# Decoder trunk with dilated attention: K and Q of a head in one transfer each, V's raw tiles ahead of them, and another order of a head's loads

## The chip, the cores and the metric

The kernel runs on one core of a Trainium2 chip. The metric is the device time of one execution in microseconds (us), lower is better. Times before are the median of three runs.

## The reference

A decoder trunk of two layers on one sequence of 1024 positions and 1024 features, in float32. Layer 0 mixes with a short gated convolution, layer 1 with dilated attention; a SwiGLU block (2816 wide) follows each, and a final RMSNorm ends it. The change lies in the attention.

```python
BRANCHES = ((128, 1), (512, 4), (2048, 16))      # window, dilation
...
def dilated_attention_mixer(h, w_qkv, w_out, rel_bias):
    qkv = (h @ w_qkv).reshape(bsz, seq, 3, N_HEADS, HEAD_DIM)   # 16 heads of 64
    q, k, v = qkv[:, :, 0], qkv[:, :, 1], qkv[:, :, 2]
    outs, lses = [], []
    for window, dilation in BRANCHES:
        o, l = dilated_branch(q, k, v, rel_bias, window, dilation)
        outs.append(o)
        lses.append(l)
    alpha = jax.nn.softmax(jnp.stack(lses, axis=0), axis=0)
    o = jnp.sum(alpha[..., None] * jnp.stack(outs, axis=0), axis=0)
    return o.reshape(bsz, seq, D_MODEL).astype(h.dtype) @ w_out
...
def dilated_branch(...):      # banded causal attention over each strided subsequence
    s = einsum(qb, kk) * (HEAD_DIM ** -0.5)
    s = where(mask, s + bias, NEG_INF)
    lse = logsumexp(s, axis=-1)
    o = einsum(exp(s - lse[..., None]), vv)
```

Query t sees the keys t - j x dilation for j = 0 to window/dilation, with a learned bias by distance and head.

## The kernel before, in words

**Numbers.** Each float32 operand of a matmul is split in two parts, hi (a copy on ScalarE, L169 for weights) and lo (a subtraction on VectorE, L170), and a product is three matmuls: hi by hi, hi by lo, lo by hi. Where the keys and queries meet, K's page holds both parts of a head (64 partitions each), so that one matmul with Q's hi part twice (L1789) and one with Q's lo part beside zeros (L1790) do it.

**Memory.** SBUF is a ring of 41 pages of 128 x 1024 float32, with half pages beside them. A tile that needs a page waits until the old holder's last reader is done. Scratch in DRAM carries the projections on: `kq[p, part]`, one tensor of 256 x 1024 for each pair of heads p and part (0 is Q, 1 is K), with the hi rows of both heads in 0 to 127 and the lo rows in 128 to 255; `vdram`, the values.

**Queues.** The order of all work is written by hand, and each engine runs its own instructions in program order. Loads are issued on SyncE (SP), in program order: a load that waits for a page holds up those behind it. Scratch stores are issued on GpSimd (POOL). Weights come as raw tiles (`load_raw`, L201 and L204), are split when `ensure` reaches them and handed out by `take`.

**Q and K.** `QueryKey` computes the projections with a seven-product scheme; `emit` writes each half page of the result as hi (L1288) and lo (L1291) to `kq`, 32 stores of each kind, between about 985 and 1105 us.

**V.** `mix` goes on with V. Its first ten heads come by seven products as well (`value_products` in the order 1, 5, 6, 7, 4, 3, 2, five of them in `mix`); the rest, the plain part of V, by eight `value_tiles` of plain matmuls, from four raw tiles of 128 x 768 numbers that come in eight transfers. Those raw tiles (index `raw_v` on) are loaded during product 3, or on demand. The loads of K and Q of head 0 (`self.first = load_rows(self, 0)`) are issued after product 4.

**Attention.** A loop over 16 heads runs `slot(n)`. Slot n issues the loads for head n + 1 (`load_kq`: K's page `ka` in two loads of 64 rows, L1240 and L1241; Q's page `qa` in two loads of the same 64 rows, one for each half of the partitions, L1243; Q's lo part `ql`, L1767; then the bias table in two loads, L1704 and L1705), computes the scores of head n (L1789, L1790, bias added on VectorE from L1800 on), starts its softmax, and multiplies the probabilities of head n - 1 with V (L1865), whose four tiles for a pair of heads (`class0`, `class1`, `keys0`, `keys1`, one buffer each) are loaded by `load_values` (L1758). ScalarE makes a regrouped copy `kca` of K (`classes`, L1773). For n below EVEN = 11 a slot is cut in eight even steps i; the value products of head n - 1 start in step 4 of slot n and end in steps 0 to 3 of slot n + 1; the V tiles of pair p are loaded in steps 0 to 3 of slot 2p + 1, in the order of VBLOCKS. From slot 11 on another order applies. Between these, `dense` work fills TensorE: the two late products of V and the value tiles, later the output projection (`out_product`), in units handed out by `other(k)`; DENSE says how many a slot gets.

The source of L1704, the bias table's first part, is a pattern `[[1, 8], [A1, 16], [1, L1]]`, that of L1705 `[[1, 32], [A2, 4], [1, L2]]`.

Of the kernel before, what the change touches and what calls it, by code (L numbers as in the profile page):

```python
# [10 lines left out]
F32 = mybir.dt.float32  # L11
# [6 lines left out]
S = 1024  # L18
D = 1024
DF = 2816  # L20
H = 16
KT = D // 128
# [50 lines left out]
EVEN, VALUES_BEFORE = 11, 17  # L73
EVEN_SOFT = (2, 1, 1, 1, 1, 1, 0, 0)
EVEN_PV = (3, 2, 2, 2, 2, 2, 2, 1)
VBLOCKS = ("class0", "class1", "keys0", "keys1")
OIN = LAG - 3
DENSE = (19, 12) + (7,) * 8 + (6, 10, 10, 12, 10, 9, 8)
DEEP_ORDER = (1, 2, 5, 6, 7, 3, 4)
# [46 lines left out]
def trunk(ctx: ExitStack, tc: tile.TileContext, x, gains_in, cwi, ck, cwo, wqkv, wo, relb,  # L126
# [19 lines left out]
    def half(h):  # L146
        return slice(h * HALF, (h + 1) * HALF)
# [44 lines left out]
    def load_raw(upto):  # L192
        while raw_state[0] < min(upto + 1, len(raw_src)):
            i, at = raw_state[0], 0
            raw_tile[i] = page("raw")
            src = raw_src[i]
            if isinstance(src, list):
                row = width(src) // 2
                for s in src:
                    n = s.shape[2]  # L200
                    nc.sync.dma_start(view(raw_tile[i], at, [[row, 2], [1, n]]), s)  # L201
                    at += n
            else:
                nc.sync.dma_start(raw_tile[i][:, :width([src])], src)  # L204
            raw_state[0] += 1
# [1022 lines left out]
    by_time = lambda t: view(t, 0, [[1, 16], [16, 32]])  # L1228
    by_residue = lambda t: view(t, 0, [[32, 16], [1, 32]])

    def rows(t, r):
        return bass.AP(t.tensor, t.offset + r * S, [[S, 64], [1, S]])

    def load_rows(qk, n):

        p, a = divmod(n, 2)
        k, q = qk.kq[p, 1], qk.kq[p, 0]
        n0, n1 = (slice(64 * i, 64 * i + 64) for i in (a, 1 - a))
        ks, qs = page("ka", F32R), page("qa", F32R)
        nc.sync.dma_start(ks[n0].bitcast(F32), rows(k, 64 * a))  # L1240
        nc.sync.dma_start(ks[n1].bitcast(F32), rows(k, 128 + 64 * a))  # L1241
        for m in (n0, n1):
            nc.sync.dma_start(qs[m].bitcast(F32), rows(q, 64 * a))  # L1243
        return ks, qs

    vdram = [dram.tile([S, w], F32, name=f"vdram{g}") for g, w in enumerate((2 * VW, VREST))]
# [1 line left out]
    class QueryKey(Conv):  # L1248
# [28 lines left out]
        def emit(self, p, part, h, v):  # L1277

            t, rstd = half_page("kq"), self.norm.rstd[:, half(h)]
            if part == 1:  # L1280
                nc.vector.tensor_tensor(out=by_time(t), in0=by_residue(v), in1=by_residue(rstd), op=ALU.mult)
            else:
                nc.vector.scalar_tensor_tensor(t, v, 0.125, rstd, op0=ALU.mult, op1=ALU.mult)
            yield
            to = self.kq[p, part]
            hi, lo = half_page("kq_hi", F32R), half_page("kq_lo", F32R)
            nc.scalar.activation(hi, t, AF.Copy)
            nc.gpsimd.dma_start(to[:128, half(h)], hi.bitcast(F32))  # L1288
            yield
            nc.vector.tensor_tensor(out=lo, in0=t, in1=hi, op=ALU.subtract)  # L1290
            nc.gpsimd.dma_start(to[128:, half(h)], lo.bitcast(F32))  # L1291

        def out(self, u, c, v):
            self.waiting.append(self.emit(u, 1 - c[0], c[1], v))
# [85 lines left out]
        def value_product(self, m, banks, ahead=0, ws=None):  # L1380

            for j in range(4):
                whi, wlo = ws[j] if ws else take(("m", ("V", j), m), ahead)
                bhi, blo = self.b[m][j]
                for t in range(4):
                    b, s, new = banks[t][:, :VW], slice(t * 128, t * 128 + 128), j == 0 and m not in (6, 7, 4)
                    nc.tensor.matmul(b, bhi[:, s], whi, start=new, stop=False, skip_group_check=True)
                    nc.tensor.matmul(b, bhi[:, s], wlo, start=False, stop=False, skip_group_check=True)
                    nc.tensor.matmul(b, blo[:, s], whi, start=False, stop=j == 3, skip_group_check=True)
                    yield  # L1390
                if m == 2 and j == 1:
                    self.stores.pop()()
                if m == 3 and j:
                    ensure(op_state[1] + j - 1)
                    load_raw(raw_v + j)
                if m == 1 or m in VALUES[:5] and j % 2:
                    self.step(1)
                if m == 6:
                    self.x12.append(half_page("x12"))
                    nc.sync.dma_start(self.x12[j], spill[j][:, half(1)])  # L1400
                elif m == 4:
                    self.operand(8, j, j, self.x12[j])
            v, c = self.v, {1: (1, 0), 5: 5, 6: (1, 1), 7: (0, 1), 4: (0, 0), 3: (1, 1), 2: (1, 0)}[m]
            if c not in v:
                v[c] = [page("v") for i in range(2)]
            part = lambda c, t: v[c][t // 2][:, half(t % 2)][:, :VW]
            for t in range(4):
                n = t + 4 * (c == 5 or c[1])
                o, scale = part(c, t), self.norm.r[:, n:n + 1]
                if m in (1, 5, 4):  # L1410
                    nc.scalar.activation(o, banks[t][:, :VW], AF.Identity, scale=scale)
                else:
                    old = part(5, t) if m in (6, 7) else o
                    nc.vector.scalar_tensor_tensor(o, banks[t][:, :VW], scale, old, op0=ALU.mult, op1=ALU.add)
            def store():
                for i in range(2):
                    self.store_values(0, v[c][i], c[1], 2 * i, c[0] * VW, VW)
                del v[c]

            if m in (3, 2):  # L1420
                self.stores.append(store)
            elif m in (7, 4):
                store()
            if m == 7:
                del v[5]
            yield
# [287 lines left out]
    def attention(norm, qk):  # L1714
# [10 lines left out]
        def value_tiles():  # L1725

            for t in range(KT):
# [15 lines left out]
                nc.scalar.activation(v[:, half(t % 2)][:, :VREST], b, AF.Identity, scale=norm.r[:, t:t + 1])  # L1743
                if t % 2:
                    qk.store_values(1, v, j, b4 - 1, 0, VREST)
                if t > KT - 3:
                    ensure(op_state[1] + t - KT + 2)
                yield
# [10 lines left out]

        def load_kq(n):  # L1760

            p, a = divmod(n, 2)
            n0 = slice(64 * a, 64 * a + 64)
            KS[n], QS[n] = load_rows(qk, n) if n else qk.first
            if EVEN + 1 < n <= LAG + 1 and n % 2 == 0:
                load_values(p - 1)
            nc.sync.dma_start(qlo[a][n0].bitcast(F32), rows(qk.kq[p, 0], 128 + 64 * a))  # L1767

        def classes(n):

# [171 lines left out]
        def slot(n, dense, ndense, late=0):  # L1942
# [10 lines left out]
            else:  # L1953
                sc = iter(())
            if n + 1 < H:
                load_kq(n + 1)
                bias[n + 1] = load_bias(n + 1)
            if n == OIN:
                for k in range(2):
                    load_x(k)  # L1960
# [19 lines left out]
            if n < EVEN:  # L1980
                for i in range(8):
# [6 lines left out]
                    other(ndense * (i + 1) // 8 - ndense * i // 8)  # L1988
                    if i == 3:
                        run(begun)  # L1990
                    if a and p and i < 4:
                        load_values(p, VBLOCKS[i:i + 1])
                    if ending and i == 4:
                        run(ending.pop())
                    if n == 0 and i == 2:
# [26 lines left out]
                        run(ending.pop())  # L2022
                run(sc)
            else:
                if a == 0 and not late:
                    other(1)
                    used += 1
                for i in range(8):
                    next(sc, None)
                    next(pv, None)  # L2030
# [53 lines left out]
                    add_to_x(n, {c: b})  # L2084

        X[:] = [None] * KT
        bias = {0: load_bias(0)}
        load_kq(0)
        late = chain(qk.late_products(), value_tiles())
        early = classes(0)  # L2090
        for i in range(VALUES_BEFORE):
# [232 lines left out]
```

## Time and profile before

| | |
|---|---|
| runs | 2072.16, 2073.15, 2073.94 us; median 2073.15 |
| profiled execution | 2074.61 us, its span 2072.8 us |
| TensorE (PE) busy | 2050.5 us (99% of the span) |
| VectorE (DVE) busy | 1806.3 us (87%) |
| ScalarE (ACT) busy | 1062.8 us (51%) |
| GpSimd (POOL) busy | 295.8 us (14%) |
| SP's hardware queue q1 | 201.15 MB, 31.9% of 16 engines' span |
| GpSimd's software queue q0 | 90.50 MB, 15.1% |

The span is that of the instructions of one profiled execution. TensorE is busy for almost all of it, so a wait elsewhere counts only where TensorE waits as well. The page names groups by line, engine, operation and tiles (`ql<-kq` is a load from `kq` into `ql`). A releaser in a row of waits is the event that came last by the profile; where several conditions share a semaphore, another may have been meant.

### The profile page before, as it was taken

The page shows a single profiled execution, that of the slowest core. Times are in us where ns is not written, and L with a number is a line of the kernel's source. Part 1 is how long each engine was busy: PE and PEld are TensorE (multiplying, and loading weights), DVE is VectorE, ACT ScalarE, POOL GpSimd, SP SyncE. Part 2 cuts the span into 40 slices and gives each one's busy share as a digit, 9 for nine tenths or more (in the row PEclk, how much of TensorE's full clock was granted, in tenths as well). Part 3 has the DMA queues.
Part 4 walks back from the last instruction along what each step waited for, and adds up shares of the span by engine and source line. Part 5 has one row for each costly group of instructions (what it writes and reads, how often), then busy time and mean ns, then how long its engine had stood idle before and what let it go on. Part 6 is the DMA issues. An engine that isn't in the chain of part 4 may idle for free.

```text
span 2072.8 us, 30544 instructions
## 1 busy us (share of the span) xinstructions
PE 2050.5 (99%) x10642; PEld 1766.4 (85%) x10642; DVE 1806.3 (87%) x3369; ACT 1062.8 (51%) x1993; POOL 295.8 (14%) x418
## 2 busy tenths in 40 slices
PE   9999999999999999999999999999999999999998
PEld 7888888888888888888889999988888888888887
DVE  8899899988888888799976999988998888897897
ACT  7433477443444555356544577665544434355444
POOL 1011011100101021020322433211011001012000
PEclk9999999999999999999999999999999999999999
DMA  7333583233333577453745978855223323378533
GB/s 223 92 111 123 158 223 72 102 112 99 115 104 105 176 237 207 157 134 111 249 163 148 236 173 212 220 173 148 71 96 104 107 97 117 102 269 225 180 98 97
DMA packets 137033, 308.30 MB, mean 149 GB/s; under 512 B 17596, under 2 KB 45582, under 8 KB 136880
## 3 DMA queue, kind: packets, MB, share of 16 engines
q1 hardware_dynamic: 96368, 201.15, 31.9%
q0 software_dynamic: 32880, 90.50, 15.1%
q10 hardware_dynamic: 7632, 14.70, 1.9%
q8 instruction: 84, 1.38, 0.3%
q14 instruction: 69, 0.57, 0.1%
HBM read 210.78 MB, written 85.29 MB: 143 GB/s over the span
## 4 chain that ended last, share of the span: by engine, by line
PE 92%; DVE 3%; DMA 3%; ACT 1%; issue 1%; SPq 0%; DVEq 0%; ACTq 0%
PE bank L652 24%; PE bank L650 24%; PE bank L651 24%; PE bank L1865 4%; PE bank L746 3%; PE bank L749 3%; PE bank L748 3%; PE bank L451 1%; PE bank L453 1%; PE bank L452 1%; PE bank L1790 1%; PE bank L1789 1%; DMA ql<-kq 1%; DMA raw<-in_conv_w_in 1%; DMA x<-in_x 0%
## 5 line engine op out<-in xcount | busy, mean ns | idle before, releaser
L650 PE MATMUL bank<-b,w 128*128 128x512 f32 (+1 forms) x2264 | 875.8, 387 | 4.0 <-ACT w L169 2.0
L652 PE MATMUL bank<-b,w 128*128 128x512 f32 (+1 forms) x2264 | 875.2, 387 | 2.1 <-DVE w L170 1.9
L651 PE MATMUL bank<-b,w 128*128 128x512 f32 (+1 forms) x2264 | 875.3, 387 | 0.3 <-DVE b L1018 0.3
L650 PEld LDWEIGHTS bank<-b,w 128*128 128x128 f32 x2264 | 425.8, 188 | 90.5 <-ACT w L169 2.4
L652 PEld LDWEIGHTS bank<-b,w 128*128 128x128 f32 x2264 | 425.7, 188 | 90.1 <-DVE w L170 4.2
L651 PEld LDWEIGHTS bank<-b,w 128*128 128x128 f32 x2264 | 425.8, 188 | 84.7 <-DVE b L1018 0.8
L169 ACT ACTIVATE w<-combo 128x512 fp32r<-128x512 f32 (+3 forms) x528 | 279.6, 555 | 293.4 <-DVE combo L242 248.5
L170 DVE TENSOR_TENSOR w<-combo,w 128x512 fp32r<-128x512 f32 (+3 forms) x528 | 309.2, 598 | 36.5 <-ACT w L169 36.1
L656 ACT ACTIVATE part<-bank 128x512 f32<-128x512 f32 x193 | 115.1, 597 | 394.1 <-PE bank L652 386.6
L170 DVE TENSOR_TENSOR w<-raw,w 128x512 fp32r<-128x512 f32 (+3 forms) x340 | 191.1, 583 | 39.6 <-ACT w L169 39.3
L660 DVE TENSOR_TENSOR part<-part,bank 128x256 f32<-128x256 f32 (+1 forms) x371 | 174.0, 498 | 31.6 <-PE bank L652 20.8
L169 ACT ACTIVATE w<-raw 128x512 fp32r<-128x512 f32 (+3 forms) x340 | 172.5, 539 | 22.3 <-PE bank L749 10.5
L642 DVE TENSOR_TENSOR b<-hin,b 128x512 fp32r<-128x512 f32 x175 | 118.7, 685 | 16.3 <-ACT b L641 14.7
L912 DVE TENSOR_TENSOR x<-x,bank 128x512 f32<-128x512 f32 x144 | 98.4, 683 | 33.5 <-PE bank L652 31.5
L242 DVE TENSOR_TENSOR combo<-raw 128x512 f32<-128x512 f32 (+2 forms) x192 | 127.4, 664 | 0.0
L641 ACT ACTIVATE b<-hin 128x512 fp32r<-128x512 f32 x175 | 107.1, 619 | 16.0 <-DMA hin<-part 11.7
L749 PE MATMUL bank<-b,w 128*128 128x256 f32 x288 | 81.5, 283 | 0.0
L748 PE MATMUL bank<-b,w 128*128 128x256 f32 x288 | 81.5, 283 | 0.0
L746 PE MATMUL bank<-b,w 128*128 128x256 f32 x288 | 81.3, 282 | 0.0
L861 POOL DMA_DIRECT2D part<-sum x88 | 47.7, 542 | 190.5 <-DVE sum L825 115.7
L1542 DVE TENSOR_TENSOR part<-part 128x512 f32<-128x512 f32 x66 | 43.5, 686 | 28.8 <-ACT part L1527 28.8
L242 DVE TENSOR_TENSOR combo<-combo,raw 128x512 f32<-128x512 f32 (+2 forms) x96 | 64.5, 672 | 3.8 <-DMA raw<-in_conv_w_in 1.0
(252 smaller groups left out, 3075.4 us busy)
## 6 DMA issues: line engine op xcount, KB each, us to landing
hin<-part SPq DMA_DIRECT2D x154, 256.0 KB
raw<-in_ffn_w_gate SPq DMA_DIRECT2D x44, 512.0 KB
raw<-in_ffn_w_up SPq DMA_DIRECT2D x44, 512.0 KB
part<-sum POOLq DMA_DIRECT2D x88, 256.0 KB, 2.3
raw<-in_ffn_w_down SPq DMA_DIRECT2D x32, 512.0 KB
raw<-in_conv_w_in SPq DMA_DIRECT2D x24, 512.0 KB
part<-part POOLq DMA_DIRECT2D x44, 256.0 KB, 2.5
raw<-in_attn_w_qkv SPq DMA_DIRECT2D x19, 512.0 KB
```

The source lines that it names most:

```text
L169: nc.scalar.activation(hi, src, AF.Copy)
L170: low = lambda: eng.tensor_tensor(out=lo, in0=src, in1=hi, op=ALU.subtract)
L242: eng.tensor_tensor(out=c, in0=a, in1=b, op=op)
L642: return lambda: eng.tensor_tensor(out=lo, in0=t, in1=hi, op=ALU.subtract)
L650: nc.tensor.matmul(b, hi[:, a], bhi, start=start and k == 0, stop=False, skip_group_check=True)
L651: nc.tensor.matmul(b, hi[:, a], blo, start=False, stop=False, skip_group_check=True)
L652: nc.tensor.matmul(b, lo[:, a], bhi, start=False, stop=k == n - 1, skip_group_check=True)
L656: nc.scalar.activation(t, b, AF.Copy)
L660: nc.vector.tensor_tensor(out=t, in0=t, in1=b, op=ALU.add)
L746: nc.tensor.matmul(b, hi[:, a], bhi, start=i in (1, 2, 5) and k == 0, stop=False, skip_group_check=True)
L748: nc.tensor.matmul(b, hi[:, a], blo, start=False, stop=False, skip_group_check=True)
L749: nc.tensor.matmul(b, lo[:, a], bhi, start=False, stop=k == n - 1, skip_group_check=True)
```

## The change

1. **Layout of `kq`.** In each 256-row tensor the rows of the first head of a pair are now hi 0 to 63, lo 64 to 127; those of the second head lo 128 to 191, hi 192 to 255. The hi store of a half page writes two blocks of 64 rows 192 rows apart, the lo store two adjoining blocks.
2. **K and Q.** A head's K page is one load of 128 adjoining rows. Its Q page is one load from a pattern that reads the same 64 rows twice, by a leading dimension of 2 with step 0.
3. **Raw tiles of V's plain part.** The four are loaded in product 4, one after each of its operand steps, and so ahead of K and Q of head 0 on SP; before, they were asked for in product 3. The raw tile after them (the first of the output projection) is asked for after the sixth value tile.
4. **V's tiles** of a pair are loaded in the order class0, keys0, class1, keys1, at steps 0, 2, 3 and 4.
5. **`ql` and the bias** get a function of their own, `load_low`. In slots 1 to 10 it is called at step 3, in later slots at the start as before; K and Q of the next head are still issued at the slot's start. All loads for heads 0 and 1 are issued before slot 0.
6. **Dense fill.** After LAG, slot 15 gets two units of `dense` work ahead of its scores and slot 16 one; before, slot 16 alone got one.

```diff
-VBLOCKS = ("class0", "class1", "keys0", "keys1")
+VBLOCKS = ("class0", "keys0", "class1", "keys1")
+VSTEP = dict(class0=0, keys0=2, class1=3, keys1=4)
...
     def load_rows(qk, n):
 
         p, a = divmod(n, 2)
         k, q = qk.kq[p, 1], qk.kq[p, 0]
-        n0, n1 = (slice(64 * i, 64 * i + 64) for i in (a, 1 - a))
         ks, qs = page("ka", F32R), page("qa", F32R)
-        nc.sync.dma_start(ks[n0].bitcast(F32), rows(k, 64 * a))
-        nc.sync.dma_start(ks[n1].bitcast(F32), rows(k, 128 + 64 * a))
-        for m in (n0, n1):
-            nc.sync.dma_start(qs[m].bitcast(F32), rows(q, 64 * a))
+        nc.sync.dma_start(ks.bitcast(F32), k[128 * a:128 * a + 128])
+        nc.sync.dma_start(qs.bitcast(F32), bass.AP(q.tensor, q.offset + 192 * a * S, [[0, 2], [S, 64], [1, S]]))
         return ks, qs
...
             nc.scalar.activation(hi, t, AF.Copy)
-            nc.gpsimd.dma_start(to[:128, half(h)], hi.bitcast(F32))
+            place = lambda r, step: bass.AP(to.tensor, to.offset + r * S + h * HALF, [[step * S, 2], [S, 64], [1, HALF]])
+            nc.gpsimd.dma_start(place(0, 192), hi.bitcast(F32))
             yield
             nc.vector.tensor_tensor(out=lo, in0=t, in1=hi, op=ALU.subtract)
-            nc.gpsimd.dma_start(to[128:, half(h)], lo.bitcast(F32))
+            nc.gpsimd.dma_start(place(64, 64), lo.bitcast(F32))
...
                 if m == 3 and j:
                     ensure(op_state[1] + j - 1)
-                    load_raw(raw_v + j)
...
                 elif m == 4:
                     self.operand(8, j, j, self.x12[j])
+                    load_raw(raw_v + j)
...
+                if t == KT - 3:
+                    load_raw(raw_v + 4)
                 if t > KT - 3:
                     ensure(op_state[1] + t - KT + 2)
...
         def load_kq(n):
 
-            p, a = divmod(n, 2)
-            n0 = slice(64 * a, 64 * a + 64)
             KS[n], QS[n] = load_rows(qk, n) if n else qk.first
             if EVEN + 1 < n <= LAG + 1 and n % 2 == 0:
-                load_values(p - 1)
-            nc.sync.dma_start(qlo[a][n0].bitcast(F32), rows(qk.kq[p, 0], 128 + 64 * a))
+                load_values(n // 2 - 1)
+
+        def load_low(n):
+
+            p, a = divmod(n, 2)
+            nc.sync.dma_start(qlo[a][64 * a:64 * a + 64].bitcast(F32), qk.kq[p, 0][64 + 64 * a:128 + 64 * a])
+            bias[n] = load_bias(n)
...
             if n + 1 < H:
-                load_kq(n + 1)
-                bias[n + 1] = load_bias(n + 1)
+                if n:
+                    load_kq(n + 1)
+                if n >= EVEN:
+                    load_low(n + 1)
...
-                    if a and p and i < 4:
-                        load_values(p, VBLOCKS[i:i + 1])
+                    if n and i == 3:
+                        load_low(n + 1)
+                    if a and p:
+                        load_values(p, [v for v in VBLOCKS if VSTEP[v] == i])
...
-                if a == 0 and not late:
-                    other(1)
-                    used += 1
+                if n >= H - 1:
+                    other(2 if n < H else 1)
+                    used += 2 if n < H else 1
...
-        bias = {0: load_bias(0)}
+        bias = {}
         load_kq(0)
+        load_low(0)
+        load_kq(1)
+        load_low(1)
```

More of the change, by code (lines that the diff above doesn't have):

```diff
@@ L1229, in trunk @@
     by_residue = lambda t: view(t, 0, [[32, 16], [1, 32]])
-    def rows(t, r):
-        return bass.AP(t.tensor, t.offset + r * S, [[S, 64], [1, S]])
     def load_rows(qk, n):
```

## The prediction

> **What bounds the kernel now.** First the page: the busy line and the chain that ended last.
>
> ```profile
> span 2072.8 us, 30544 instructions
> PE 2050.5 (99%) x10642; PEld 1766.4 (85%) x10642; DVE 1806.3 (87%) x3369; ACT 1062.8 (51%) x1993; POOL 295.8 (14%) x418
> PE 92%; DVE 3%; DMA 3%; ACT 1%; issue 1%; SPq 0%; DVEq 0%; ACTq 0%
> ```
>
> TensorE is busy for 99% of the span, so a change of loads can win only idle time of TensorE or time at a lower clock. All that the change touches lies between 985 and 1392 us, so I next asked for windows there. Their columns are start:end, length, busy time of each engine, granted clock, busy share of the 16 DMA engines, and GB/s.
>
> ```profile
> core 0: us, PE busy (x) PEld busy (x) DVE busy (x) ACT busy (x) POOL busy (x), PEclk, DMA share, GB/s
> 18.00:22.00 4.00, 4.00 (x20) 3.30 (x19) 2.70 (x5) 2.03 (x4) 0.00 (x0) 1.00 1.04 410
> 985.00:1105.00 120.00, 119.47 (x539) 98.96 (x539) 104.90 (x166) 55.47 (x98) 34.56 (x64) 1.00 0.63 212
> 1141.16:1153.51 12.35, 12.06 (x88) 11.85 (x87) 9.12 (x19) 4.50 (x5) 6.05 (x9) 1.00 1.07 308
> 1153.51:1292.89 139.38, 133.29 (x1028) 130.97 (x1027) 137.78 (x266) 95.70 (x145) 51.70 (x43) 0.99 0.80 195
> 1292.89:1364.75 71.86, 71.86 (x504) 66.39 (x502) 62.14 (x124) 43.22 (x66) 20.30 (x12) 1.00 0.74 207
> ```
>
> A head's slot begins with its first product of K and Q (L1789). The second window is the store stage of K and Q, the third is slot 0, the fourth slots 1 to 10, the fifth slots 11 to 14:
>
> ```profile
> 1141.16 0.28 PE L1789 MATMUL bank<-qa,kca 128*128 128x256 f32 x1
> 1153.51 0.28 PE L1789 MATMUL bank<-qa,kca 128*128 128x256 f32 x1
> 1292.89 0.28 PE L1789 MATMUL bank<-qa,kca 128*128 128x256 f32 x1
> 1364.75 0.28 PE L1789 MATMUL bank<-qa,kca 128*128 128x256 f32 x1
> ```
>
> Slots 1 to 10 take 139.38/10 = 13.94 us each. In them VectorE is busy for 137.78 us of 139.38, and the DMA engines for 0.80 of the time on average. Three resources are close to full, and TensorE's waits are small. The waits of TensorE from 1100 to 1400 us, and VectorE's longest from 1140 to 1320 us (total, times, longest):
>
> ```profile
> PE bank L1865 <- DMA v_class<-vdram: 2.4, 3, 1.6
> PE bank L1790 <- DMA ql<-kq: 1.7, 2, 1.2
> PE bank L1865 <- ACT o L1888: 1.4, 1, 1.4
> PE bank L1865 <- ACT lf L1854: 0.9, 1, 0.9
> PE bank L1789 <- DMA qa<-kq: 0.4, 1, 0.4
> PE bank L1790 <- DMA raw<-in_attn_w_qkv: 0.3, 1, 0.3
> ...
> DVE w_lo L170 <- DMA ql<-kq: 1.7, 1, 1.7
> ```
>
> That is 7.1 us in all. The third is a wait for `v_keys` as well: in the program the instruction needs that load and a tile of exponentials, and ACT's `o` only shares its semaphore. Slots 1 to 10 also lose to the clock, after the longest wait for `ql`:
>
> ```profile
> 1168.59 0.39 PE L1790 MATMUL bank<-ql,kca 128*128 128x256 f32 x1 [1.19 <-DMA ql<-kq]
> 1168.00:1170.00 2.00, 1.41 (x9) 1.41 (x10) 2.00 (x6) 1.98 (x5) 1.92 (x1) 0.83 1.04 228
> 1170.00:1172.00 2.00, 2.00 (x11) 2.00 (x11) 1.97 (x4) 0.89 (x2) 1.11 (x1) 0.50 0.79 184
> 1172.00:1174.00 2.00, 2.00 (x16) 2.00 (x15) 2.00 (x5) 0.69 (x2) 1.04 (x1) 0.82 0.85 158
> ```
>
> Three windows of 2 us at 0.83, 0.50 and 0.82 lose (0.17 + 0.50 + 0.18) x 2 = 1.7 us. So everything that better loads could give is 7.1 + 1.7 = 8.8 us, less what VectorE takes in their place.
>
> **Merged K and Q (the part that decides).** SP's issues for head 0, with start and duration, and the page's sizes:
>
> ```profile
> 1128.72 0.54 SPq L1240 DMA_DIRECT2D ka<-kq  x1
> 1129.94 1.24 SPq L1243 DMA_DIRECT2D qa<-kq  x2
> 1136.35 5.76 SPq L201 DMA_DIRECT2D raw<-in_attn_w_qkv  x8
> ...
> ka<-kq SPq DMA_DIRECT2D x32, 256.0 KB
> qa<-kq SPq DMA_DIRECT2D x32, 256.0 KB
> ```
>
> Four issues become two, which saves 0.54 + 0.62 = 1.2 us of SP per head. I cost it at nothing: SP is not what TensorE waits for, and the bytes are the same. K is then one load whose source leads with 128 rows. Q is different. It must land twice, once for each half of the partitions, and the new source says so with a leading dimension of 2 (step zero), ahead of 64 rows. What does a short leading dimension cost? One load of the kernel has one: L1704, the first part of the bias table, leads with 8; the second part, L1705, leads with 32. The last pair of them stands alone on SP's queue for over 11 us:
>
> ```profile
> 1342.37 0.62 SPq L1704 DMA_DIRECT2D bias<-tables  x1
> 1343.04 0.55 SPq L1705 DMA_DIRECT2D bias<-tables  x1
> 1354.43 0.55 SPq L1758 DMA_DIRECT2D v_class<-vdram  x1
> ...
> 1344.00:1346.40 2.40, 2.40 (x21) 2.27 (x20) 2.40 (x5) 1.02 (x2) 1.54 (x1) 1.00 1.03 230
> 1346.50:1347.50 1.00, 1.00 (x11) 1.00 (x10) 1.00 (x2) 0.97 (x3) 0.00 (x0) 1.00 0.55 96
> 1347.50:1348.50 1.00, 1.00 (x8) 0.87 (x7) 1.00 (x3) 1.00 (x3) 0.00 (x0) 1.00 0.50 164
> ```
>
> While the older loads drain, all engines are busy (1.03). Then the share falls to 0.55 and 0.50 and stays there: half of the engines go on, the others have nothing left. I read this as L1704 handed out by its leading dimension, 8 pieces to 8 of 16 engines. By the same reading Q's load goes to 2 engines. The bounds are 16 engines (like the 64-row loads) and 2; the nearest row is L1704's, so I take 2.
>
> The Trainium skill, "DMA: Bandwidth & Descriptors", section "Rules for kernel authors", states this outright: a leading zero-stride broadcast of c copies confines a transfer to at most c engines. The 0.50 above agrees for c = 8; no run shows c = 2 yet. By the page's remark there that two transfers to disjoint partition halves should be one 128-partition transfer, the merge of Q would cost nothing; the row speaks for the first rule.
>
> The price: the first window moves 410 GB/s at a full share, 410/(16 x 1.04) = 24.6 GB/s per engine, on weight rows as long as Q's (4 KB). Q writes 2 x 262,144 bytes. Over 16 engines that is 32,768 bytes or 1.33 us of each; over two, 262,144 bytes or 10.65 us of each. These two must also carry their sixteenth of all else. In slots 1 to 10 that is 195 GB/s x 139.38 us / 16 / 10 = 169.9 KB per head, less 32.8 KB of Q as it is now: 137.1 KB. At 24.6 GB/s it takes 5.6 us; at the stretch's own 195/16/0.80 = 15.2 GB/s, 9.0 us; at the rate of the half-busy window, 164/(16 x 0.50) = 20.5 GB/s, 6.7 us. I take the last, since that window holds the same short rows (bias) as most of this traffic. A head then needs 10.65 + 6.7 = 17.3 us of the two engines (16.2 to 19.7), against 13.94 now. Each slot needs the Q that was issued a slot earlier, and every load spread over 16 engines ends with its slowest part, so the slots run at the pace of the two: 10 x (17.3 - 13.94) = **+34 us** (23 to 58).
>
> Slots 11 to 14: their engines each move 207 x 71.86/16 = 930 KB, less 4 x 32.8 = 799 KB, or 39 us at 20.5 GB/s, and four Qs 42.6 us: 82 us in 71.9. But a part of it (weights, x) is prefetch that may be late, and slot 11's own V has 20 us of slot to land in; I take **+4** (0 to 10). Slot 15 loads no Q, and catches the remainder up.
>
> **Raw tiles of V's plain part sooner.** Eight issues (5.76 us of SP) move from behind K and Q of head 0 to ahead of them; they hold four pages earlier, which the earlier part can spare at best. 4 x 128 x 768 x 4 bytes = 1.57 MB, 98 KB per engine, 4.0 us. It removes the 0.3 us wait on `raw` and VectorE's 1.7 us before `w_lo` (put down to `ql`, but that split needs `raw`). K and Q of head 0 now stand behind them. K was issued at 1128.72; the old raw issues were spread to 1142.1 by pages coming free, so sooner issues are held by the same pages, and I put the first free time of the two engines at about 1138. Q of head 0 lands at about 1149, and with K's copy on ACT slot 0 starts near 1150 instead of 1141.2: +9. Behind it lie `ql` and bias of head 0 and K of head 1 (some 70 KB per engine, 2.9 us), and then Q of head 1 (10.65): slot 1 starts near 1164.5 instead of 1153.5. So the lead-in is **+11 us** in all (9 to 16).
>
> **Low parts, bias and V's blocks.** `ql` and bias move from a slot's start to its step 3, behind Q of the next head and, in odd slots, ahead of `class1` and `keys1`. V's blocks come as class0, keys0, class1, keys1. What goes with it are the waits of 2.4, 1.7 and 1.4 us. With spread loads these would go; with the two slow engines the same loads queue behind 10.65 us of Q, so they turn up again as waits inside the same 17.3 us: nothing beside the sum. The half clock of 1.7 us also lies within slots that the two engines set.
>
> **Store layout.** The stores keep their bytes and number; hi now leads with 2 instead of 128, lo is one block of 128 rows:
>
> ```profile
> kq<-kq_hi POOLq DMA_DIRECT2D x32, 256.0 KB, 3.5
> kq<-kq_lo POOLq DMA_DIRECT2D x32, 256.0 KB, 3.1
> ```
>
> On two engines a hi store takes 131,072/24.6 GB/s = 5.3 us instead of 0.67. If successive stores take different engines, the 120 us of this stage carry the same total, and the last ones end well before K's first load at 1128.72: zero. If always the same two, see the rivals. No row shows a POOL transfer with a short lead; between the ends I take zero.
>
> **Dense fill.** Slot 15 gets two units and slot 16 one. TensorE does the same work; the 0.9 us wait for ACT's `lf` is covered: **-1 us**.
>
> **Sum.** 34 + 4 + 11 - 1 = +48 us. The profiled execution took 2074.61 us, 1.8 us over its span of 2072.8 and 1.46 over the median of the runs, 2073.15. So 2074.6 + 48 = 2122.6 for such an execution, and 2073.15 + 48 = about **2121 us** for the median.
>
> **Rivals.**
>
> *Q's load uses all 16 engines* (faster). For it: the 64-row loads now do, and they cover the same partitions. Against it: the 0.50 of L1704. Then Q costs 1.33 us per engine as before, and V, `ql` and raw come sooner. Of 8.8 us, VectorE, with 1.6 us idle in slots 1 to 10, keeps some: at least 4 come through, so I put it at -6: about 2067 us (2064 to 2069).
>
> *The hi stores pile up on the same two engines* (slower still). 32 x (5.33 - 0.67) = 149 us more for these two, on top of 0.63 x 120 = 76 us busy: 225 us of work against 120 us of stage and the 24 us to K's load: +82, and with head 0's loads behind that backlog some 130 us over before: about 2205 us. Against it: that two engines are chosen once and for all is an assumption.
>
> The page named above, section "Why a DMA increments its semaphore by 16 and not by 1", says that GpSimd's transfers take consecutive engines from a round-robin cursor, which speaks against this rival; no row shows it.
>
> *Two engines, but hidden* (no change). Slots would need 13.9 us or less of them: the rest of a head's traffic in 3.3 us, that is 42 GB/s per engine, over the 24.6 of any row. I see no way but a gain elsewhere that happens to cancel.
>
> **How the numbers follow.** The forecast gets 0.83: it rests on one reading of a share that fell to a half. All 16 engines get 0.10, the pile-up 0.05, no change 0.02. The forecast's own range: low ends 23 + 0 + 9 - 1 = +31; high ends 58 + 10 + 16 = +84; if Q's rows, too, move at 20.5 GB/s (12.8 us), ten heads add 22, together +106 at the very most. I take 2100 to 2170 for it, and the same as the range, which leaves out the 0.10 below and 0.05 above. 0.2% (4.1 us) is about what a measurement can tell from no change: faster 0.10, same 0.02, slower 0.88.
>
> **What would show it.** Right: slots 1 to 10 about 17 us apart, TensorE waiting several us in nearly each of them for `qa`, `ql` or `v_class`, the DMA share there falling with GB/s near 160 (27.2 MB in 173 us), ACT's copy of K waiting less than L1789 does. Slot 0 near 1150. The raw and `lf` waits gone. `kq_hi` landing later than 3.5 us while `kq_lo` stays near 3.1, and no new waits in 985 to 1128. Wrong: slots near 12.9 to 13.5 us with no wait for `qa` (16 engines), or K's first load far behind 1128 (pile-up). The size is wrong if Q lands faster than in 10 us, or if the slots hide more than the pace of the two engines allows.

## The result, and the profile after

The changed kernel takes 2170.6 us (median of four runs, 2166.7 to 2173.76) against 2073.47 for the kernel before, measured beside it: ratio 1.0469, 95% interval 1.0449 to 1.0488, **97 us slower**. The forecast was 2121 us with a range of 2100 to 2170. The direction was right, and so was what it said of Q's load; the size was half of what came, the stores of K and Q, which it put at nothing, took their part of it, and the time lies just outside the range. The profiled execution took 2169.07 us.

The changed kernel's page, as far as it answers to the lines shown of before:

```profile
span 2167.3 us, 30465 instructions
PE 2077.4 (96%) x10642; PEld 1785.0 (82%) x10642; DVE 1809.2 (83%) x3369; ACT 1062.0 (49%) x1993; POOL 305.6 (14%) x418
q1 hardware_dynamic: 95632, 201.15, 29.7%
q0 software_dynamic: 47216, 90.62, 15.6%
PE 82%; DMA 12%; DVE 3%; issue 2%; ACT 1%; POOL 0%; SPq 0%; DVEq 0%; POOLq 0%; ACTq 0%
```

The bytes are the same (201.15 MB on SP's queue), but DMA has gone from 3% to 12% of the chain that ended last. TensorE's busy time has risen by 27 us with the same 10642 matmuls; some of them are seen below at half clock. To say where the 97 us arise, take the same matmuls in both traces. First the first product of V, between 1080 and 1130 us (after the count min/median/max ns, then first and last start). Before:

```profile
L1387 PE MATMUL bank<-w,b x71: 305/309/309, 1098.9 to 1129.7; 128*128 128x320 f32 x71
```

and after:

```profile
L1383 PE MATMUL bank<-w,b x29: 305/309/309, 1116.0 to 1129.7; 128*128 128x320 f32 x29
```

Then the starts of slots 0, 1, 11 and 15 after (1141.16, 1153.51, 1292.89 and 1364.75 before):

```profile
1168.56 0.55 PE L1790 MATMUL bank<-qa,kca 128*128 128x256 f32 x1 [8.76 <-DMA qa<-kq]
1183.75 0.36 PE L1790 MATMUL bank<-qa,kca 128*128 128x256 f32 x1 [0.68 <-DMA qa<-kq]
1374.90 0.58 PE L1790 MATMUL bank<-qa,kca 128*128 128x256 f32 x1 [4.81 <-ACT kca L1774]
1459.98 0.28 PE L1790 MATMUL bank<-qa,kca 128*128 128x256 f32 x1
```

The kernel is behind by 17.1 us at the first V product, 27.4 at slot 0, 30.2 at slot 1, 82.0 at slot 11 and 95.2 at slot 15. So 17 us are lost up to the end of the store stage of K and Q, another 13 in the lead-in to slot 1, 52 in slots 1 to 10 and 13 in slots 11 to 14; then the distance is nearly constant (the span is 94.5 us longer).

The matmuls of the two traces, taken in order, show where the 17 us come from. 1.5 of them are there by 100 us, ahead of all that was changed. The rest arises in the first part of the store stage, in 197 matmuls that before took 45.00 us (columns as in the prediction):

```profile
995.00:1040.00 45.00, 44.88 (x197) 36.46 (x197) 44.83 (x70) 23.80 (x41) 17.34 (x33) 1.00 0.80 271
```

The same 197 after, with ScalarE's longest wait among them:

```profile
996.50:1057.05 60.55, 52.02 (x197) 39.26 (x196) 46.06 (x71) 22.99 (x41) 22.61 (x33) 0.92 0.70 187
ACT kq_hi L1282 <- DMA kq<-kq_hi: 23.6, 7, 6.0
```

That is 15.55 us more; from there to 1102 us of the trace before the distance stays the same. Before, VectorE was busy for 44.83 of the 45.00 us: it had no time to spare there. After, ScalarE waits for half pages that hi stores still hold, and TensorE for ScalarE (`part`) and VectorE (`w`). TensorE's longest waits from 950 to 1500 us in the changed kernel:

```profile
PE bank L1866 <- DMA v_class<-vdram: 39.1, 6, 9.1
PE bank L1790 <- DMA qa<-kq: 17.6, 4, 8.8
PE bank L651 <- ACT part L657: 5.4, 3, 3.5
PE bank L1790 <- ACT kca L1774: 4.8, 1, 4.8
PE bank L653 <- DVE w L171: 3.1, 4, 1.6
```

and three of its windows, with the columns as before:

```profile
1183.77:1374.98 191.21, 142.62 (x1027) 139.54 (x1027) 133.80 (x254) 92.66 (x139) 51.91 (x43) 0.86 0.51 140
1255.00:1257.00 2.00, 2.00 (x16) 1.79 (x14) 1.97 (x5) 1.71 (x3) 0.82 (x1) 1.00 0.13 51
1288.00:1292.00 4.00, 4.00 (x34) 4.00 (x33) 3.97 (x8) 2.72 (x5) 0.00 (x0) 1.00 0.13 52
```

Slots 1 to 10 now run at 140 GB/s and a DMA share of 0.51, where before they ran at 195 and 0.80. The last two windows each lie in the landing of one Q load and show only that: the share is 0.13, two of 16 engines (0.125), and they move 51 to 52 GB/s, 26 GB/s each. That is the step on which the forecast stood, now seen directly, and the rule of the Trainium skill ("DMA: Bandwidth & Descriptors", section "Rules for kernel authors") agrees for c = 2 as it did for 8. The longest group of waits is not for Q itself but for V's blocks. They are issued after it, and their patterns lead with 128, so by the same reading a part of each stands behind Q on the two engines.

TensorE also runs slowly after a long wait: its clock is 0.50 from 1236.1 to 1240.1 us, after a wait for `v_class`, and so it is after the 8.76 us wait of slot 0:

```profile
1168.56:1170.56 2.00, 1.29 (x4) 1.02 (x5) 0.00 (x0) 0.00 (x0) 0.00 (x0) 0.50 0.72 176
1170.56:1172.56 2.00, 2.00 (x10) 2.00 (x9) 1.57 (x4) 0.00 (x0) 0.00 (x0) 0.50 0.59 161
1172.56:1174.56 2.00, 2.00 (x18) 2.00 (x16) 1.21 (x3) 1.76 (x3) 0.00 (x0) 0.96 0.14 55
```

### The profile page after: what moved, and what is told of

It is laid out like the page before. It is cut to its first block, busy times and chain, and to the rows that moved or that the text cites. A ratio compares the mean times of both kernels' runs of the same rounds, so it can differ in the third digit from the quotient of the medians.

```text
span 2167.3 us, 30465 instructions
## 1 busy us (share of the span) xinstructions
PE 2077.4 (96%) x10642; PEld 1785.0 (82%) x10642; DVE 1809.2 (83%) x3369; ACT 1062.0 (49%) x1993; POOL 305.6 (14%) x418
## 3 DMA queue, kind: packets, MB, share of 16 engines
q1 hardware_dynamic: 95632, 201.15, 29.7%
q0 software_dynamic: 47216, 90.62, 15.6%
## 4 chain that ended last, share of the span: by engine, by line
PE 82%; DMA 12%; DVE 3%; issue 2%; ACT 1%; POOL 0%; SPq 0%; DVEq 0%; POOLq 0%; ACTq 0%
PE bank L651 22%; PE bank L653 22%; PE bank L652 22%; DMA v_class<-vdram 3%; PE bank L747 3%; PE bank L750 3%; PE bank L749 3%; DMA ql<-kq 3%; PE bank L1866 3%; DMA raw<-in_attn_w_qkv 1%; DMA bias<-tables 1%; DMA raw<-in_attn_w_out 1%; PE bank L452 1%; PE bank L454 1%; PE bank L453 1%
## 5 line engine op out<-in xcount | busy, mean ns | idle before, releaser
L653 PEld LDWEIGHTS bank<-b,w 128*128 128x128 f32 x2264 | 427.0, 189 | 95.2 <-DVE w L171 8.0
L642 ACT ACTIVATE b<-hin 128x512 fp32r<-128x512 f32 x175 | 107.2, 619 | 15.6 <-DMA hin<-part 9.8
L1866 PE MATMUL bank<-lf,v_class 128*128 128x128 f32 x256 | 41.3, 311 | 39.8 <-DMA v_class<-vdram 39.1
L1866 PEld LDWEIGHTS bank<-lf,v_class 128*128 128x128 f32 x256 | 37.7, 222 | 42.0 <-issue 37.4
```

The lines of the kernel that those rows point to most:

```text
L653: nc.tensor.matmul(b, lo[:, a], bhi, start=False, stop=k == n - 1, skip_group_check=True)
L1866: nc.tensor.matmul(view(acc[ih], off, dims), v[:, u * 192 + 128 * a:u * 192 + 128 * a + 128], rhs, start=first, stop=last)
```

## The experiments

All were timed against the kernel before on the same chip, whose median was 2074.02 us beside the first four kernels below, 2074.24 beside Q led by 4, no bias loads, raw tiles late and the old order, 2073.39 beside only Q, more half pages, the old fill and only the early loads, and 2074.48 beside the hi stores led by 4. These medians differ by up to 1.1 us from chip to chip, so a difference between two kernels of different groups is uncertain by about as much.

**Q in two loads.** The changed kernel, with this one edit:

```diff
-        nc.sync.dma_start(qs.bitcast(F32), bass.AP(q.tensor, q.offset + 192 * a * S, [[0, 2], [S, 64], [1, S]]))
+        for m in (slice(0, 64), slice(64, 128)):
+            nc.sync.dma_start(qs[m].bitcast(F32), q[192 * a:192 * a + 64])
```

> Only Q's load is undone: two loads of 64 adjoining rows, each with 64 as its leading dimension; all else as in the changed kernel. Theory A (Q's load sits on two of 16 engines): what was lost from slot 0 on comes back. By matching matmuls one by one, the changed kernel lost 11.9 us from the last V products to slot 1, 51.8 us in slots 1 to 10 and 11.7 us after, 75 us in all; so about 2170.6 - 75 = 2095 us, and up to 6 less if the waits of the kernel before go too (2088 to 2097). The 16.7 us lost while K and Q are stored stay. Rival B (the new order of ql, bias and V's blocks is what starves TensorE): within 10 us of 2170.

Measured 2086.67 us, ratio 1.0056 (1.0043 to 1.0069). 84 of the 97 us are gone. Theory A holds, though the time lies 1 us below its range, and the rival on the order falls: the order is still there.

**Hi in two stores.** The changed kernel, Q still one load:

```diff
-            nc.gpsimd.dma_start(place(0, 192), hi.bitcast(F32))
+            for i in range(2):
+                nc.gpsimd.dma_start(to[192 * i:192 * i + 64, half(h)], hi[64 * i:64 * i + 64].bitcast(F32))
```

> Only the hi store is undone: two stores of 64 rows each instead of one led by a 2; Q's load stays on its leading 2. Theory A: the 16.7 us lost in the store stage (about 1000 to 1110 us) come back, 2170.6 - 16.7 = about 2154 us (2151 to 2157), hi stores land near 3.5 us, the 8-byte packets (47216 - 32880 on the software queue) vanish. Rival B (the stage is late for another reason, such as GpSimd's longer issues, 829 ns against 540): 32 more issues of some 540 ns make it no better, about 2168 to 2175 us. Rival C (hidden behind the loads of head 0 anyhow): same as the changed kernel.

Measured 2151.84 us, ratio 1.0374 (1.036 to 1.0388): 18.8 us back. The count, size and median time to landing of the stores in the changed kernel:

```profile
kq<-kq_hi POOLq DMA_DIRECT2D x32, 256.0 KB, 11.2
kq<-kq_lo POOLq DMA_DIRECT2D x32, 256.0 KB, 10.8
```

and in this one:

```profile
kq<-kq_hi POOLq DMA_DIRECT2D x64, 128.0 KB, 3.5
kq<-kq_lo POOLq DMA_DIRECT2D x32, 256.0 KB, 3.0
```

Theory A holds, and up to 1130 us the matmuls of this kernel run within 0.1 us of those of the kernel before. A hi store led by 2 landed in 11.2 us instead of 3.5, and the lo stores between landed later as well. GpSimd now spends more time on its issues (64 hi stores of 532 ns instead of 32 of 829), and nothing is lost by it, so its issue time was not the cause.

**Both undone.** The two edits together.

> Both undone, the rest of the change kept (K in one load, raw tiles sooner, new order, dense fill). Theory A: both losses go, 97 us, and of the 8.8 us of waits and low clock in the kernel before some 4 to 8.8 go too: 2064 to 2069 us. Rival B (losses overlap, something else in the change costs): over 2075 us.

Measured 2069.27 us, ratio 0.9976 (0.9967 to 0.9985): faster than both kernels. 2170.6 - 2069.3 = 101.3 us, close to 83.9 + 18.8, so the two losses add. Of the 97 us lost, the rest of the change had given 4.8 back. TensorE's waits from 1100 to 1420 us are now

```profile
PE bank L1868 <- ACT lf L1857: 0.5, 1, 0.5
PE bank L1868 <- DVE lp L1834: 0.4, 1, 0.4
PE bank L1868 <- ACT o L1891: 0.3, 1, 0.3
PE bank L1868 <- DVE lf L1803: 0.2, 1, 0.2
PE bank L1868 <- ACT ld L1857: 0.2, 1, 0.2
PE bank L1868 <- ACT lp L1857: 0.2, 1, 0.2
```

1.8 us instead of 7.1, and no DMA among them.

**Only the order.** The kernel before with its layout, its four loads of K and Q and its stores; only parts 3 to 6 of the change (`ql` from row 128 + 64a, as the layout has it).

> The kernel before with its layout and its four loads for K and Q, and only the moves: raw tiles sooner, V's blocks, ql and bias later, dense fill. Theory A (merging K saves only issue time of SP, which nothing waits for): the same as the kernel with both undone within 2 us, 2064 to 2070 us. Rival (K's one load and the fewer issues matter, since SP waits for the transfer eight issues before): 3 to 6 us slower than that one.

Measured 2069.18 us, ratio 0.9975 (0.9966 to 0.9983). Merging K brings nothing that can be measured beside it; the gain is in parts 3 to 6.

**Q led by 4.** From the kernel with hi in two stores:

```diff
-        nc.sync.dma_start(qs.bitcast(F32), bass.AP(q.tensor, q.offset + 192 * a * S, [[0, 2], [S, 64], [1, S]]))
+        for m in (slice(0, 64), slice(64, 128)):
+            nc.sync.dma_start(qs[m].bitcast(F32), bass.AP(q.tensor, q.offset + 192 * a * S, [[S, 4], [4 * S, 16], [1, S]]))
```

> From the kernel with hi stored in two: Q in two loads again, but each source leads with 4 instead of 64 (64 rows as 4 times every fourth row, so Q's rows come in another order than K's, and the scores are not the reference's). Theory A (a load uses as many engines as its leading dimension, and the slots run at the pace of the fullest engine): Q takes 4 x 32,768 = 131 KB of each of four engines per head, 5.3 us, and the rest of a head 7.3 us more with the bias part that leads with 8, times 19.1/17.9, the measured pace over the same sum for two engines: 13.4 us per head, as long as a slot of the kernel with both undone (134 us for ten). So most of the 82.6 us between 2151.8 and 2069.3 are gone: 2069 to 2080 us. Rival B (Q's own time to land counts, and it halves): 2069 + 41 = about 2110 us.

Measured 2086.72 us, ratio 1.0066 (1.0049 to 1.0083): 17.4 over the kernel with both undone, between the two expectations and nearer to A; B's 2110 is far off. Its slots 1 to 10 start at

```profile
1160.98 0.28 PE L1792 MATMUL bank<-qa,kca 128*128 128x256 f32 x1
1302.21 0.39 PE L1792 MATMUL bank<-qa,kca 128*128 128x256 f32 x1 [2.06 <-ACT kca L1776]
```

and last 141.23 us, 14.1 each against the 13.4 expected. The expectation had left out the lead-in: slot 1 starts 7.8 us later than with both undone (1153.20), about as much as the slots lose (7.1). From two engines to four the loss falls from 82.6 us to 17.4, far more than by half, as it must where most of it is what exceeds a slot's own length.

**No bias loads.** From the kernel with hi in two stores and Q led by 2, the bias tile of head 0 is kept for all heads, so that the scores are not the reference's:

```diff
-            bias[n] = load_bias(n)
+            bias[n] = (first_bias or first_bias.append(load_bias(n)) or first_bias)[0]
...
-        bias = {}
+        bias, first_bias = {}, []
```

> From the kernel with hi stored in two, Q still led by 2: the bias table is loaded for head 0 only and used for all heads (15 pairs of bias loads left out). Theory A (the slots run at the pace of the two engines, all their work counts): per head 184,832/8 + 178,688/16 bytes = 34 KB less on them, 1.4 us at 24.6 GB/s to 1.7 at 20.5, for some 14 heads: 20 to 24 us less, 2128 to 2132 us. Rival B (the slots are set by Q alone and by TensorE's half clock after each wait): 2146 us or more.

Measured 2132.28 us, ratio 1.0279 (1.0265 to 1.0293): 19.6 us less. The starts of slots 1 and 11 with hi in two stores:

```profile
1166.39 0.28 PE L1791 MATMUL bank<-qa,kca 128*128 128x256 f32 x1
1356.66 0.58 PE L1791 MATMUL bank<-qa,kca 128*128 128x256 f32 x1 [4.57 <-ACT kca L1775]
```

and without bias loads as well:

```profile
1166.87 0.28 PE L1791 MATMUL bank<-qa,kca 128*128 128x256 f32 x1
1342.25 0.58 PE L1791 MATMUL bank<-qa,kca 128*128 128x256 f32 x1 [3.96 <-ACT kca L1775]
```

190.27 us become 175.38: 1.49 us a slot for 34 KB less on each of the two engines, 23 GB/s. That is the price of these bytes on the two engines, and rival B falls: the slots run at the pace of these two, and the bytes of the bias count on them beside Q's. The run also takes two issues a head off SP, which it can't tell apart from the bytes.

**Only Q.** The kernel before, with Q's load led by 2 and nothing else:

```diff
-        for m in (n0, n1):
-            nc.sync.dma_start(qs[m].bitcast(F32), rows(q, 64 * a))
+        nc.sync.dma_start(qs.bitcast(F32), bass.AP(q.tensor, q.offset + 64 * a * S, [[0, 2], [S, 64], [1, S]]))
```

> The kernel before with one edit: Q's two loads of 64 rows become one that leads with a 2. Theory A: the loss from slot 0 on comes by itself, whatever the order of the other loads: the two engines need 19.1 us per head against 13.9, +52 in slots 1 to 10, some 8 in the lead-in (Q of head 0 isn't behind V's raw tiles here) and 12 after: 2074 + 72 = about 2146 us (2135 to 2155). Rival (the new order made it worse than it had to be): under 2125 us.

Measured 2172.92 us, ratio 1.0478 (1.0463 to 1.0492): 99.5 us, as much as the whole change. That one line carries a loss of this size by itself; but the expectation was 27 us short. In the old order slots 1 to 10 take 203.70 us:

```profile
1170.41 0.42 PE L1788 MATMUL bank<-qa,kca 128*128 128x256 f32 x1 [4.83 <-DMA qa<-kq]
1374.11 0.58 PE L1788 MATMUL bank<-qa,kca 128*128 128x256 f32 x1 [6.65 <-ACT kca L1772]
```

20.4 us each against 19.0 in the new order, with the same bytes. The wait for V is longer here than in the kernel with hi in two stores, whose row follows it:

```profile
PE bank L1864 <- DMA v_class<-vdram: 46.5, 6, 10.3
```

```profile
PE bank L1867 <- DMA v_class<-vdram: 39.5, 6, 9.2
```

So the bytes on the two engines aren't all; what is queued ahead of V on them is the likely rest. The new order, which one rival blamed, softens the loss in the slots. Of what the expectation missed, about 9 us lie before slot 1 (16.9 us late instead of 8), 12 in slots 1 to 10 (64.3 us more than before instead of 52) and 4 in slots 11 to 14 (16 more instead of 12). Which load's place makes them was not tried apart.

**More half pages.** From the kernel with Q in two loads (hi still led by 2): PAGES 39 instead of 41, and 24 half pages instead of 20 in the first and third pool.

> From the kernel with Q in two and hi still led by a 2 (2086.7 us): 24 half pages instead of 20, paid for by 39 pages instead of 41. Theory A (the store stage is late because hi's half pages stay occupied for 11 us instead of 3.5 and ScalarE waits for one, 8 waits and 28.7 us): 64 stores held some 8 us longer in 120 us are 4.3 half pages more on average, so four more give back most of the 17 us in this stage, at least 10; pages missing elsewhere may cost some of it again: 2071 to 2080 us. Rival B (GpSimd's longer issues or the engines' load are what it waits for): the stage stays 15 to 17 us late, 2086 or more.

Measured 2103.08 us, ratio 1.0138 (1.0122 to 1.0153): slower, and the expectation missed. ScalarE's waits for a `kq_hi` half page from 985 to 1110 us, with 20:

```profile
ACT kq_hi L1283 <- DMA kq<-kq_hi: 30.1, 9, 7.2
```

and with 24:

```profile
ACT kq_hi L1283 <- DMA kq<-kq_hi: 5.4, 1, 5.4
```

These waits almost went, but the stage gave back only some 5 us (by the same matmuls, those at 994 and 1102 us in the kernel before, it lost 17.1 us in the one and 11.9 in the other). Two pages less cost more than that elsewhere: it is 4 us late at 994 us already, and from 1102 us to slot 0 it loses 8 us more. So ScalarE's wait for `kq_hi` is not the whole of it; the stage lies between what theory A and rival B expected.

**Hi stores led by 4.** From the kernel with only the order:

```diff
-            nc.gpsimd.dma_start(to[:128, half(h)], hi.bitcast(F32))
+            nc.gpsimd.dma_start(bass.AP(to.tensor, to.offset + h * HALF, [[S, 4], [4 * S, 32], [1, HALF]]), hi.bitcast(F32))
```

> From the kernel with only the order changed (2069.2 us): the hi store leads with 4 (4 times every fourth row, 32 of them, so hi's rows come in another order and the scores are not the reference's). Led by 2, a store landed in some 11 us, and the stage lost 17; led by 128, in 3.5, and it lost nothing. Theory A (the time to land, that is the number of engines, sets the loss through the half pages held): four engines move 65,536 bytes each, 2.7 us at 24.6 GB/s instead of 5.3, landing near 5 to 6 us, a quarter of the extra hold, loss 0 to 5 us: 2069 to 2074. Rival B (GpSimd's longer issue and the small packets cost, whatever the number of engines): 10 us or more, 2079 and up.

Measured 2080.1 us, ratio 1.0031 (1.0017 to 1.0046): 10.9 us over its base, and the stores land later than expected:

```profile
kq<-kq_hi POOLq DMA_DIRECT2D x32, 256.0 KB, 8.7
kq<-kq_lo POOLq DMA_DIRECT2D x32, 256.0 KB, 7.6
```

By bytes per engine the landing was expected at 5 to 6 us. Theory A's numbers don't hold; rival B's time does (10 us or more, 2079 and up). Of B's two causes the issue time fell with hi in two stores, but the small packets remain: a lead of 4 brings fewer of them than a lead of 2 (the last section has the counts), and no run has few engines without small packets. In the four kernels the loss goes with the time to land: a lead of 128 (3.5 us) costs 0, of 4 (8.7 us) 10.9, of 2 (11.2 us in the changed kernel) 17.4 us, the last by the kernel with Q in two loads. Whether few engines or small packets make the landing late, and by which buffer it comes to TensorE, stays open.

**V's raw tiles late.** From the kernel with both undone, `load_raw(raw_v + j)` back in product 3 and the later call removed.

> From the kernel with both undone: V's raw tiles asked for in product 3 again, as in the kernel before. In the kernel before the waits on raw were 0.3 us on TensorE and 1.7 us on VectorE. Theory A: 0.5 to 2 us slower than 2069.3, 2070 to 2071 us. Rival: K and Q of head 0 come sooner and nothing is lost, 2069 us.

Measured 2078.94 us, ratio 1.0021 (1.0012 to 1.0031): 9.7 us slower, five times the expectation. With head 1's loads now also ahead of slot 0, the raw transfers stand behind them on SP:

```profile
1141.36 8.69 SPq L202 DMA_DIRECT2D raw<-in_attn_w_qkv  x6
```

and the loss arises in slot 0: slot 1 starts at 1162.65 us instead of 1153.20. One wait of TensorE, put down by the profile to a bank's reader, makes up most of it:

```profile
PE bank L1790 <- DVE lf L1801: 6.9, 1, 6.9
```

**Old order of ql, bias and V.** From the kernel with both undone, V's blocks in the old order and steps and `load_low(n + 1)` at the slot's start.

> From the kernel with both undone: ql and bias issued at the slot's start again and V's blocks in the old order and steps. Theory A (the gain on the kernel before is mostly V's and ql's waits): 2 to 4 us slower, 2071 to 2073 us. Rival B (the gain comes from all of head 1's loads going ahead of slot 0, which stays here): within 1 us of 2069.3.

Measured 2069.47 us, ratio 0.9977 (0.9969 to 0.9985): the same as with them, as rival B expected, though 3.0 us of waits for `v_class` are back. Why those waits cost nothing was not tested; VectorE, which was busy for 137.78 of 139.38 us in these slots before, may be what they wait beside.

**Old dense fill.** From the kernel with both undone, `other(1)` at the start of slot 16 alone.

> From the kernel with both undone: the dense fill of the kernel before (one unit at the start of slot 16, none ahead of slot 15). Theory A (it covers the 0.9 us wait for lf in slot 15): 0 to 1 us slower, 2069 to 2071 us, which hardly shows beyond the interval. Rival: over 2 us slower.

Measured 2069.8 us, ratio 0.9982 (0.9973 to 0.9991); the `lf` wait is 0.9 us again instead of 0.5. No difference that can be told.

**Only the early loads.** The kernel before with V's raw tiles in product 4 and all loads of heads 0 and 1 ahead of slot 0.

> The kernel before with its own layout, four loads, V order, ql and bias at the slot's start and dense fill, and only V's raw tiles in product 4 and all loads of heads 0 and 1 ahead of slot 0. Theory A (the 4.8 us won on the kernel before come from the first slots, where ql of heads 1 and 2 and raw were late): 2069 to 2071 us. Rival B (each part has a share): 2072 to 2074 us.

Measured 2073.08 us, ratio 0.9996 (0.9987 to 1.0005): theory A falls, and the time is inside rival B's range. The raw, `ql` and `qa` waits go, but

```profile
PE bank L1871 <- DMA v_class<-vdram: 3.4, 3, 1.7
PE bank L1871 <- ACT lf L1860: 3.0, 3, 1.8
```

stand in their place. The early loads came to 2069 us with the new order and the fill (only the order), with K's merge and the fill (old order), and with K's merge and the new order (old fill). So they need company, but no one part of it is needed in all three; more was not taken apart.

## Why the prediction was right or wrong

That Q's load would sit on two engines and set the pace was foreseen. Two steps failed: the store layout, put at nothing, and the price of a slot, put at 17.3 us.

*Two engines.* Right, and shown: a share of 0.13 in Q's landings, 84 us back with Q's load alone undone, 99.5 lost with it alone made. The row it was read from was thin: the half share lasted 2 us, and the next microsecond shows 0.16.

*Q's price, 10.65 us.* Right where Q runs alone (51 to 52 GB/s over two engines make 10.1 to 10.3 us of 524,288 bytes).

*The slots, 17.3 us, +34.* The direction was right, but this is the term that was mis-sized most in us: 191.15 us for ten, 19.1 each, +52. The working gave the bias load the same sixteenth as the rest, though the argument itself rested on that load being on 8 engines; that is 11.6 KB or 0.5 us a head more. The rest, 1.3 us a head, is inside the stated bound of 19.7, and its cause stays open: the run without bias loads shows that the pace is that of these engines, at 23 GB/s for the bytes taken off, and the run with Q alone that bytes aren't all.

*Store layout, zero.* Wrong. The step took "the same total over changing engines" for "no cost". The total is the same, and the loads of head 0 found no backlog such as the rival of the pile-up had: the DMA engines are idle from 1134 to 1138 us, and K is issued at 1149. But each hi store landed 7.7 us later, and the lo stores, which were to stay near 3.1 us, landed in 10.8. ScalarE waited for the half pages that they held, in a stretch in which VectorE had no time to spare; 15.6 us were lost in the stage, and 18.8 came back when the hi store was undone. By the run with more half pages that wait is not the whole way by which the loss comes to TensorE. Of the two bounds named, the truth lay between, and the text had no row for the time to land of a store with a short lead.

*Lead-in, +11.* 13 us (30.2 less 17.1), slot 0 +10.3 against the +9 forecast. Right, and with hi in two stores it is the same: slot 1 starts 12.9 us later than before.

*Slots 11 to 14, +4.* 13 us. Here the sum itself had 82 us of work in 71.9, +10, and it was discounted as prefetch that may be late. Taken whole, that sum would have come near. With both undone these slots take 73.6 us against 71.9 before, so 1.7 of the 13 don't come from the two patterns; they are the order's.

*Dense fill, -1, and the order.* The fill is worth nothing measurable. The waits named do go with the order, and the gain, 4.8 us, which shows once the two patterns led by 2 are undone, lies in the lower part of the 4 to 8.8 us that the rival with 16 engines named. But it is not the sum of these waits: with the old order of `ql`, the bias and V 3.0 us of them come back, and the time stays the same.

*No cost of the half clock beside the sum.* The windows after slot 0's wait lose 2.1 us to it. That it adds nothing in slots that the two engines set was argued and not shown; it is part of the 27 us by which TensorE's busy time rose, and was not measured apart.

The sum with the measured terms is 17 + 13 + 52 + 13 - 1 = 94 us of span, against 48 forecast; 1.5 of the 17 are there ahead of the stage, and the 1 is made good after slot 15's start (95.2 us late there, 94.5 at the end). The text's own worst case was +106 us, or 2179; its range stopped at 2170 and gave no reason.

## What to carry to other kernels

Look at the outermost dimension of both sides of a transfer before you merge two into one: a leading 2 here put Q's load on two of 16 engines and cost 84 to 99.5 us, while merging K's two loads, which saved an issue of SP, was worth nothing measurable. When a share of DMA drops to 2/16 or 8/16 with work still queued, count engines, and price a transfer by what the fullest engine has to carry, other loads included. Price the time to land of a store as well as its bytes: the buffer it frees is somebody's next input.

## What the runs showed of the hardware that was not expected

GpSimd's stores led by 2 bring small packets: SP's queue has about as many packets as before, but the software queue goes from 32880 to 47216, and its bytes only from 90.50 to 90.62 MB, some 8 bytes for each new packet. That is 448 more for each of 32 stores; with a lead of 4 the count is 39024, 192 more for each. The counts are 14 x 32 and 12 x 16, multiples of the engines that a lead of 2 or 4 would leave unused; what the packets are for, no run shows. An issue takes longer too. Before:

```profile
L1288 POOL DMA_DIRECT2D kq<-kq_hi x32: 540/542/564, 991.4 to 1102.3; - x32
```

After, with the time to landing of the hi stores:

```profile
L1284 POOL DMA_DIRECT2D kq<-kq_hi x32: 829/829/846, 992.9 to 1119.4; - x32
DMA to landing us min/median/max: 8.6/11.2/15.2
```

No landing took more than 15.2 us, though 32 stores at 5.3 us, the prediction's estimate, would be 170 us of work on one pair of engines, and the stores were issued within 127 us; so they do not all go to the same two. The Trainium skill ("DMA: Bandwidth & Descriptors", section "Why a DMA increments its semaphore by 16 and not by 1") has GpSimd's transfers that use fewer than 16 engines take consecutive ones in turn; the landing agrees. No stretch of these traces shows such a store alone, so that it uses two engines is read from Q's load and not seen.
